# Later sums of squares for the norms behind the feed-forward blocks, and one set of squares for two norms between the layers

## The chip, the core and the metric

The kernel runs on one core of one Trainium2 chip. The metric is the device time of one execution in microseconds (us); the time before is the median of three runs. The core has five engines that work side by side, each through its own list of instructions in order: TensorE (PE in the profile, its weight loads PEld), VectorE (DVE), ScalarE (ACT), GpSimd (POOL) and SyncE (SP, which issues DMAs here; POOL issues some too). An instruction that waits for another engine holds up all that stands behind it on its own.

## The reference

Two layers over x of 512 tokens by 1024 features, in float32:

```
for l in range(2):
    x = x + 0.5 * swiglu(rms_norm(x, ffn1_norm[l]), gate1, up1, down1)     # "FFN1", inner width 2816
    h = rms_norm(x, mix_norm[l]); p = h @ w_in[l]                           # "mix": latent attention and a conv module
    x = x + concat(attention(p), conv(p)) @ w_out[l]
    x = x + 0.5 * swiglu(rms_norm(x, ffn2_norm[l]), gate2, up2, down2)     # "FFN2"
    x = rms_norm(x, post_norm[l])
rms_norm(x, g) = x * rsqrt(mean(x*x over features) + 1e-6) * g
```

Between the layers two norms follow each other: the post norm of layer 0 and the FFN1 norm of layer 1.

## The kernel before, in words

x lies in on-chip memory turned, as 8 tiles `x[:, m, :]` of 128 features by 512 tokens. Every float32 product is made of three cheaper ones of 512 (or 256) columns (`mm3`, lines 208 to 213): high part times high part, high times low, low times high. So each operand is split into a high part (an ACT cast, line 158 for a weight, 297 for a feed-forward quarter) and a low part (a DVE subtraction, lines 165 and 299). A weight arrives in a `raw` buffer by DMA, is cast, and its low part follows.

**Norms.** A product may start before the norm's factor is known: the operand is x times the gain (`split_scaled`, lines 223 and 224), and the products are multiplied by the factor afterwards. The factor takes these steps, in class `Stats` and its users:
- `add`: ACT squares an x tile (line 243; line 240 for the first, into the accumulator) and DVE or POOL adds it to the accumulator (line 247);
- `sums`: four one-column products on PE (line 254) sum the accumulator over the features;
- `token`: DVE scales the sums (`vtok`, line 261), POOL raises them to the power -0.5 (`rtok`, line 229); a first call of `norm()` does this much;
- `spread_sb`: four transposes on PE (line 270) spread the 512 factors over all partitions, an ACT copy (line 276) brings them to R; this is the second call of `norm()`.

Between the layers `NormPost` does it for two norms: it has two accumulators (st3 for x, st4 for x times the post gain), two sets of sums, a chain of small DVE and POOL steps (lines 1245 to 1251), and two spreads (R and Rp).

**A feed-forward block** (`ffn_body`) works on 11 pairs of inner column groups, in chunks (0,2), (2,5), (5,8), (8,11). Chunk 0 uses plain products: pair 0, then pair 1, each in two rows r, each row with two banks of PSUM (gate and up) of 24 products. When R is there, `plain_out` (lines 352 to 357) makes an activation of a row's two banks, split at lines 217 and 218; four activations come out of chunk 0. At the same time the generator `operands` (lines 375 to 388) prepares the operands of the other chunks on DVE and ACT. Chunk 0's down projection starts three blocks "ahead" with the first three activations. Chunks 1 to 3 use a seven-product scheme over three pairs each (`pair`, `down`), and the last `down` calls `done` for each finished x tile; the squares come behind that.

**The mix** (`mix_body`) starts with two groups of 24 products from the conv weights `wcv` (variable `first`), then one group from `wql` (step q0), then R, then the next conv groups (step c1, weights `wcv` again), and so on after the list `SEQ`.

**Order.** The program is recorded in the order of the code; a scheduler then sets each engine's order by its own timing, with a limited number of buffers per pool (7 PSUM banks). `tc.issue_after(i)` adds the condition that what is recorded under it stands behind instruction i on the same engine. `in_turn` (lines 181 to 184) keeps the low parts on DVE in their order by such a condition: `turns[V]` is the instruction behind which the next low part stands.

Of the kernel before, what the change touches and what calls it, by code (L numbers as in the profile page):

```python
# [12 lines left out]
ALU = mybir.AluOpType  # L13
# [48 lines left out]
WOG = 4  # L62
CHAIN = 400
WAKE = 10
KS = (0, 2, 4, 6, 1, 3, 5, 7)
WOP = 4
EVP = "DAD"
# [17 lines left out]
def encoder_kernel(ctx: ExitStack, tc: tile.TileContext, xT, consts, vecs, rgain, wgu1, wd1, wdq1,  # L85
# [21 lines left out]
    def bank():  # L107
        return psum.tile([P, S], FP, tag="ps", name=nm("ps"))
# [122 lines left out]
    class Stats:  # L231
# [5 lines left out]
        def add(self, src, scale=1.0, last=False, eng=None, apart=False, into=None):  # L237
            if self.acc is None:
                self.acc = slot() if into is None else into
                A.activation(self.acc, src, AF.Square, scale=scale)  # L240
                return
            sq = tmp() if into is None else into
            A.activation(sq, src, AF.Square, scale=scale)  # L243
            if apart:
                self.tail = sq
                return
            (eng or (V if last else G)).tensor_tensor(self.acc, self.acc, sq, ALU.add)

        def sums(self, made=bank):
            ps = made()  # L250
# [56 lines left out]
    def ffn_body(fpool, l, gx, norm, wgu, wd, wdq, wdr, gain, done, w0, halved, chunks, whole, late_rows):  # L307
# [52 lines left out]
        def after(name):  # L360
            return tc.issue_after(order[name]) if name in order else nullcontext()
# [199 lines left out]
        def advance(n):  # L561
            for _ in range(n):
                next(steps, None)

        for p0, p1 in chunks:
            f0, fn = 2 * p0, 2 * (p1 - p0)
            last = p1 == NF // 2
            short = last and p0 == CHUNKS[-1][0]
            act = held if short else []
            for p in range(p0, p1) if not short else ():  # L570
                if p == 0:
                    os = []
                    for r in range(2):
                        ws = w0[2 * r:2 * r + 2] if w0 else [load_w(wgu[l, p, 2 * r + q], WC) for q in range(2)]
                        os.append([bank(), bank()])
                        if w0 and not r:
                            plain_first(os[r], ws)
                        elif w0:
                            plain(os[r][:1], ws, range(KD))
                            plain([None] + os[r][1:], ws, range(KD // 2))  # L580
                            with tc.issue_after(order["mm"]):
                                norm()
                            with after("sums"):
                                plain([None] + os[r][1:], ws, range(KD // 2, KD))
                        elif late_rows:
                            for a, b in WHOLE:
                                plain(os[r], ws, range(a, b))
                                if r and a == 0:
                                    with tc.issue_after(order["mm"]):
                                        norm()  # L590
                            if r:
                                R = norm()
                        else:
                            plain(os[r], ws, range(KD - 1))
                            plain(os[r], ws, range(KD - 1, KD))
                            R = norm()
                    if not w0:
                        scaled(os, R)
                elif p < CHUNKS[0][1]:
                    for r in range(2):  # L600
                        ws = [load_w(wgu[l, p, 2 * r + q], WC) for q in range(2)]
                        o = [bank(), bank()]
                        if w0 and not r:
                            with tc.issue_after(order["mm"]):
                                plain(o[:1], ws, KS[:KD // 4])
                            with tc.issue_after(order["mm"]):
                                R = norm()
                            with after("spread"):
                                plain(o[:1], ws, KS[KD // 4:])
                                plain([None] + o[1:], ws, range(KD))  # L610
                            scaled(os, R)
                        else:
                            plain(o, ws, range(KD))
                        advance(8)
                        act.append(plain_out(o, R))
                else:
                    order.setdefault("pe", order["mm"])
                    act += pair(p, whole or not last)
            if p0 and (whole or not last):
                c = (p0 - CHUNKS[0][1]) // NP  # L620
                if p1 == CHUNKS[-1][0]:
                    held = pair(p1, False)
                down(act, (lambda g: wdq[l, g, c]) if p1 - p0 == NP else (lambda g: wdr[l, g]), done if last else None)
                continue
            ahead = {}
            if short:
                wide_w = [load_cols(wd, l, 4 * q, f0, fn) for q in range(2)]
            def block(m, queue=None):
                return load_w(wd[l, m, :, f0 * P:(f0 + fn) * P], fn * P, queue=queue)
            if p0 == 0:  # L630

                for m in range(3):
                    ahead[m] = bank(), block(m, G)
                    group(*ahead[m], act, range(fn - 1), fn)
                next_w = {3: block(3, G)}
            for m in range(halved if last else KD):
                if short:
                    pd = bank()
                    group(pd, part_w(wide_w, m, fn), act, range(fn), fn)
                elif m in ahead:  # L640
                    pd, w = ahead[m]
                    group(pd, w, act, range(fn - 1, fn), fn)
                else:
                    pd = bank()
                    w = next_w[m] if p0 == 0 else block(m)
                    group(pd, w, act, range(fn), fn)
                if p0 == 0 and m + 4 < KD:
                    next_w[m + 4] = block(m + 4, G)
                    if m == 0:
                        order["low"] = turns[V]  # L650
                if p0 == 0:
                    advance(2)
                    if norm.after:
                        with tc.issue_after(order["evicted"]):
                            norm.after(m)
                with after("low") if m in ahead and m else nullcontext():
                    order["evicted"] = V.scalar_tensor_tensor(x[:, m, :], pd, 0.5, x[:, m, :], ALU.mult, ALU.add).ins
                if last:
                    done(m)
            if last:  # L660

                ms = range(halved, KD)
                ws = [part_w(wide_w, m, fn) if short else load_w(wd[l, m, :, f0 * P:(f0 + fn) * P], fn * P) for m in ms]
                for h in range(2):
                    ts = slice(h * HS, (h + 1) * HS)
                    for m, w in zip(ms, ws):
                        pd = bank()
                        group(pd[:, 0:HS], w, act, range(fn), fn, ts)
                        V.scalar_tensor_tensor(x[:, m, ts], pd[:, 0:HS], 0.5, x[:, m, ts], ALU.mult, ALU.add)
                        done(m, h)  # L670
            if p0 == 0:
                advance(99)
# [10 lines left out]
            mix_body(kpool, l, gx, norm, done)  # L683

    def mix_body(kpool, l, gx, norm, done):
        u, order = [], {}
        diag = kpool.tile([P, PT, Q], FP, tag="m", name=nm("m"), bufs=11)
        G.tensor_tensor(diag, cst[:, None, CI32:CI32 + Q].to_broadcast([P, PT, Q]),
                        vv(l, "cp")[:, :, None].to_broadcast([P, PT, Q]), ALU.mult)
# [53 lines left out]
        ssk = small.tile([P, NT, H], FP, tag="ssk", name=nm("ssk"))  # L743

        def latent_q(j):
            ps = bank()
            group(ps, load_w(wql[l, j], WC, "q"), gx, range(KD), KD)
            pq.append(ps)

        def latent_q_out():  # L750
# [127 lines left out]


        first = groups([wcv[l, 0], wcv[l, 1]], gx, WHOLE)  # L880
        rm = norm()
        for step in SEQ.split():
            if step == "R":
                R = norm()
# [327 lines left out]
    for l in range(L):  # L1212
# [10 lines left out]
        if l + 1 < L:  # L1223
            nx, st4 = [], Stats()
            gc = tiny("gc", KD)
            G.tensor_tensor(gc, gp, vv(l + 1, "g1"), ALU.mult)

            def done2(m):
                nx.append(split_scaled(x[:, m, :], gc[:, m:m + 1]))
                for i in range(KD) if m == KD - 1 else ():  # L1230
                    with tc.issue_after(order["scaled"]):
                        st3.add(x[:, i, :], eng=V)
                        A.activation(x[:, i, :], x[:, i, :], AF.Copy, scale=gp[:, i:i + 1])
                        st4.add(x[:, i, :], eng=V)
            ffn(l, gx, norm2, wgu2, wd2, wdq2, None, vv(l, "g2"), done2, chunks=SHORT, whole=True)
            gx = nx

# [125 lines left out]
```

## Time and profile before

| | us |
|---|---|
| median of three runs (1743.22 to 1745.96) | 1745.44 |
| the profiled execution | 1745.87 |
| its span, first to last instruction | 1743.7 |
| PE busy in the span | 1723.4 (99%) |
| DVE / ACT / POOL busy | 1482.4 / 1111.3 / 365.0 |

Times in the profile count from the span's start. The 2.2 us between the execution's time and its span lie outside of the instructions. An engine's busy time is the union of its instructions; PE's instructions overlap their neighbours, so a busy PE is not a PE at its peak, and the granted clock (PEclk, 1.00 is full) has to be read beside it. The rows read "start, duration, engine, line, operation, out<-in, size", and a bracket tells how long the engine sat idle before and what released it.

### The profile page before, as it was taken

How to read it: one execution, taken by the hardware profiler on the slowest of the kernel's cores; microseconds unless marked ns; L12 is line 12 of the kernel's file. 1: busy time of each engine (PE TensorE's matmuls, PEld its weight loads, DVE VectorE, ACT ScalarE, POOL GpSimd, SP SyncE). 2: the span in 40 equal slices, each digit the busy share in tenths (PEclk: the TensorE clock that was granted, in tenths of full speed). 3: DMA queues.
4: the chain of work that ended last, by engine and by line, in shares of the span. 5: the costliest groups of instructions: out<-in, count | busy, mean ns of one | idle time of the engine just before them, and what ended most of it. 6: DMA issues, size and time to landing. Idle time of an engine off the chain costs nothing. (4 is left out here: it accounts for less than half of the span.)

```text
span 1743.7 us, 31890 instructions
## 1 busy us (share of the span) xinstructions
PE 1723.4 (99%) x12684; PEld 1586.6 (91%) x12684; DVE 1482.4 (85%) x2145; ACT 1111.3 (64%) x1727; POOL 365.0 (21%) x334
## 2 busy tenths in 40 slices
PE   9999999999999999999999999999999999999998
PEld 8899999888678899999979999998976788999997
DVE  7888989978965989898988989897989659888887
ACT  5576757557953576757755757675778435767564
POOL 2000000047823100010010011110576410011110
PEclk9999999999999999999999999999999999999999
DMA  5567575424303466676525575754251125675743
GB/s 184 146 154 196 134 201 132 141 73 120 75 25 103 115 166 173 160 176 160 137 74 156 133 199 132 202 132 132 83 151 32 51 83 149 157 190 138 199 110 100
DMA packets 73269, 234.21 MB, mean 134 GB/s; under 512 B 8736, under 2 KB 10912, under 8 KB 73120
## 3 DMA queue, kind: packets, MB, share of 16 engines
q1 hardware_dynamic: 51984, 163.48, 29.2%
q0 software_dynamic: 20992, 68.69, 21.8%
q8 instruction: 99, 1.62, 0.4%
q14 instruction: 50, 0.41, 0.1%
q10 hardware_dynamic: 144, 0.00, 0.0%
HBM read 227.95 MB, written 2.10 MB: 132 GB/s over the span
## 5 line engine op out<-in xcount | busy, mean ns | idle before, releaser
L211 PE MATMUL ps<-r,weights 128*128 128x256 f32 (+1 forms) x2680 | 819.2, 306 | 0.0
L210 PE MATMUL ps<-r,weights 128*128 128x256 f32 (+1 forms) x2680 | 814.8, 307 | 0.3 <-ACT weights L297 0.2
L212 PE MATMUL ps<-r,weights 128*128 128x256 f32 (+1 forms) x2400 | 739.1, 310 | 1.1 <-DVE weights L299 1.1
L210 PEld LDWEIGHTS ps<-r,weights 128*128 128x128 f32 x2680 | 504.9, 188 | 30.0 <-ACT weights L158 1.7
L211 PEld LDWEIGHTS ps<-r,weights 128*128 128x128 f32 x2680 | 505.0, 188 | 26.7 <-DVE r L224 0.2
L212 PEld LDWEIGHTS ps<-r,weights 128*128 128x128 f32 x2400 | 451.6, 188 | 30.3 <-DVE weights L299 1.5
L210 PE MATMUL ps<-xj,weights 128*128 128x256 f32 x864 | 238.5, 276 | 0.0
L211 PE MATMUL ps<-xj,weights 128*128 128x256 f32 x864 | 238.5, 276 | 0.0
L297 ACT CAST weights<-fr 128x1024 fp32r<-128x1024 f32 (+2 forms) x184 | 175.9, 956 | 90.3 <-DVE fr L452 44.9
L299 DVE TENSOR_TENSOR weights<-fr,weights 128x1024 fp32r<-128x1024 f32 (+2 forms) x184 | 203.8, 1107 | 31.1 <-ACT weights L297 31.1
L158 ACT CAST weights<-raw 128x1024 fp32r<-128x1024 f32 (+4 forms) x116 | 105.5, 922 | 165.7 <-PE ps L211 95.1
L432 POOL DMA_DIRECT2D ls<-in_wgu x72 | 62.9, 873 | 581.7 <-ACT ls L431 526.4
L165 DVE TENSOR_TENSOR weights<-raw,weights 128x1024 fp32r<-128x1024 f32 (+4 forms) x100 | 107.0, 1080 | 65.1 <-ACT weights L158 64.8
L210 PEld LDWEIGHTS ps<-xj,weights 128*128 128x128 f32 x864 | 162.2, 188 | 0.0
L211 PEld LDWEIGHTS ps<-xj,weights 128*128 128x128 f32 x864 | 162.2, 188 | 0.0
L212 PE MATMUL ps<-xj,ls 128*128 128x256 f32 x576 | 159.0, 276 | 0.0
L297 ACT CAST weights<-raw 128x1024 fp32r<-128x1024 f32 (+2 forms) x116 | 110.2, 950 | 45.6 <-DVE raw L535 26.6
L299 DVE TENSOR_TENSOR weights<-raw,weights 128x1024 fp32r<-128x1024 f32 (+2 forms) x116 | 127.8, 1101 | 12.9 <-ACT weights L297 12.5
L1028 POOL TENSOR_TENSOR y<-y,pr 128x495 f32<-128x495 f32 (+29 forms) x90 | 119.3, 1328 | 51.9 <-ACT pr L1026 46.6
L431 ACT ACTIVATE ls<-fr 128x1024 fp32r<-128x1024 f32 (+2 forms) x64 | 62.5, 976 | 103.8 <-PE ps L212 65.1
L519 DVE SCALAR_TENSOR_TENSOR x<-ps,x 128x512 f32<-128x512 f32 x168 | 115.1, 685 | 5.7 <-PE ps L212 4.9
L432 POOL DMA_DIRECT2D ls<-in_wdq x44 | 38.3, 871 | 343.1 <-ACT ls L431 326.3
(259 smaller groups left out, 3083.8 us busy)
## 6 DMA issues: line engine op xcount, KB each, us to landing
fr<-in_wgu SPq DMA_DIRECT2D x112, 512.0 KB, 4.6
ls<-in_wgu POOLq DMA_DIRECT2D x72, 512.0 KB, 7.3
raw<-in_wgu SPq DMA_DIRECT2D x62, 512.0 KB, 5.1
fr<-in_wdq SPq DMA_DIRECT2D x66, 384.0 KB, 4.8
ls<-in_wdq POOLq DMA_DIRECT2D x44, 384.0 KB, 6.2
raw<-in_wdq SPq DMA_DIRECT2D x22, 384.0 KB, 5.6
raw<-in_wd POOLq DMA_DIRECT2D x32, 256.0 KB, 3.1
raw<-in_wcv SPq DMA_DIRECT2D x16, 512.0 KB, 3.3
```

Of the source, the lines that this page charges most:

```text
L158: order["cast"] = in_turn("h", lambda: A.copy(hi[:, :w], raw[:, :w]))
L165: in_turn(e, lambda: e.tensor_tensor(lo[:, :w], raw[:, :w], hi[:, :w].bitcast(FP), ALU.subtract))
L210: T.matmul(o, lh, rh, start=first, stop=False, skip_group_check=free)
L211: T.matmul(o, lh, rl, start=False, stop=False, skip_group_check=free)
L212: order["mm"] = T.matmul(o, ll, rh, start=False, stop=last, skip_group_check=free).ins
L297: in_turn("h", lambda: A.copy(hi[:, :w], src[:, :w]))
L299: order["lo"] = in_turn(V, lambda: V.tensor_tensor(lo[:, :w], src[:, :w], hi[:, :w].bitcast(FP), ALU.subtract))
L431: A.activation(lo[:, :n], src[:, :n], AF.Copy, scale=-1.0)
L432: G.dma_start(out=lo[:, :n], in_=w, accum_op=ALU.add)
L519: return V.scalar_tensor_tensor(v, o.rearrange("p (m t) -> p m t", m=2), 0.5 * sign, v, ALU.mult, ALU.add).ins
L1028: order["conv"] = G.tensor_tensor(ys[c][:, s:], ys[c][:, s:], pr[:, s:], ALU.add).ins
```

## The change

Three places, one idea: the sums of a norm's squares stand further back in PE's order, with products of the next group ahead of them and behind them, before the spread.

- In the mix, `norm()` is no longer called after the two first conv groups. Step q0 records four of its eight k-steps (QS = 4, twelve products), then the sums behind them, then the other twelve, and the spread of step R follows. `turns[V] = summed` puts the low parts of all weights loaded after q0's behind the last addition of squares on DVE.
- In FFN1 of layer 1 (`late_rows`), the sums stand twelve products earlier than the end of pair 0 (after LS = 6 of 8 k-steps of row 1), and the spreads move from behind pair 0 into pair 1, behind 18 products of its first bank. `scaled` (the first two `plain_out` and the start of `operands`) follows there.
- Between the layers one set of ACT squares serves both accumulators: st4 adds the square times gp*gp (`add_scaled`, DVE). The second set of eight squares goes; the eight scalings of x by gp (line 1233) stay.

```diff
+QS = 4
+LS = 6
 class Stats:
     def add(...):
...
-            (eng or (V if last else G)).tensor_tensor(self.acc, self.acc, sq, ALU.add)
+            self.last = (eng or (V if last else G)).tensor_tensor(self.acc, self.acc, sq, ALU.add).ins
+            return sq
+
+        def add_scaled(self, sq, scale):
+            if self.acc is None:
+                self.acc = slot()
+                V.tensor_scalar(self.acc, sq, scale, None, ALU.mult)
+            else:
+                self.last = V.scalar_tensor_tensor(self.acc, sq, scale, self.acc, ALU.mult, ALU.add).ins
 ffn_body:
+        early = w0 or late_rows
...
                         elif late_rows:
                             for a, b in WHOLE:
-                                plain(os[r], ws, range(a, b))
-                                if r and a == 0:
+                                if r and a == LS:
                                     with tc.issue_after(order["mm"]):
                                         norm()
-                            if r:
-                                R = norm()
+                                with after("sums") if r and a == LS else nullcontext():
+                                    plain(os[r], ws, range(a, b))
...
-                    if not w0:
+                    if not early:
                         scaled(os, R)
...
-                        o = [bank(), bank()]
-                        if w0 and not r:
+                        o = [bank()]
+                        if not (late_rows and not r):
+                            o.append(bank())
+                        if early and not r:
+                            n = LS if late_rows else KD // 4
                             with tc.issue_after(order["mm"]):
-                                plain(o[:1], ws, KS[:KD // 4])
+                                plain(o[:1], ws, KS[:n])
                             with tc.issue_after(order["mm"]):
                                 R = norm()
+                            if late_rows:
+                                o.append(bank())
                             with after("spread"):
-                                plain(o[:1], ws, KS[KD // 4:])
+                                plain(o[:1], ws, KS[n:])
 mix_body, latent_q(j):
             ps = bank()
-            group(ps, load_w(wql[l, j], WC, "q"), gx, range(KD), KD)
+            w = load_w(wql[l, j], WC, "q")
+            if not j:
+                turns[V] = summed
+                group(ps, w, gx, range(QS), KD)
+                with tc.issue_after(order_of("product")):
+                    rm = norm()
+            with tc.issue_after(order_of("sums")) if not j else nullcontext():
+                group(ps, w, gx, range(0 if j else QS, KD), KD)
...
-        rm = norm()
+        rm, summed = None, norm.st.last
 between the layers:
+            gp2 = tiny("gp2", KD)
+            G.tensor_tensor(gp2, gp, gp, ALU.mult)
...
-                        st3.add(x[:, i, :], eng=V)
+                        sq = st3.add(x[:, i, :], eng=V)
+                        st4.add_scaled(sq, gp2[:, i:i + 1])
                         A.activation(x[:, i, :], x[:, i, :], AF.Copy, scale=gp[:, i:i + 1])
-                        st4.add(x[:, i, :], eng=V)
```

How the instructions stand then, at the places that the prediction speaks of (the changed file's lines are numbered from 2 on, in these functions 10 to 23, higher; L210, L211, L212 of before are L212, L213, L214 there).

PE at the start of the mix in layer 0, before: ps_3965 and ps_3966 are the banks of the two first conv groups, r_3902 the accumulator of squares, ps_4024 the bank of q0.

```order
L210 MATMUL ps_3966<-r_3898,weights 128x512
...
L212 MATMUL ps_3966<-r_3898,weights 128x512
L254 MATMUL ps_4016<-ones,r_3902 128x1 x4
L210 MATMUL ps_4024<-r_3869,weights 128x512
...
L212 MATMUL ps_4024<-r_3898,weights 128x512
L270 MATMUL ps_4053<-cst,rtok_4022 128x128 x4
```

The same place in the changed kernel; q0's bank is ps_4015.

```order
L214 MATMUL ps_3966<-r_3898,weights 128x512
L214 MATMUL ps_4015<-r_3873,weights 128x512
...
L214 MATMUL ps_4015<-r_3881,weights 128x512
L264 MATMUL ps_4033<-ones,r_3902 128x1 x4
L212 MATMUL ps_4015<-r_3885,weights 128x512
...
L214 MATMUL ps_4015<-r_3898,weights 128x512
L280 MATMUL ps_4053<-cst,rtok_4039 128x128 x4
```

The sums stood behind the last product of the first groups with all 24 of q0 between them and the spread; now twelve of q0's products stand ahead of the sums and twelve behind.

DVE at that place, before: r_3895 and r_3899 are the low parts of the last two x tiles, raw_4025 is q0's weight, raw_4069 and raw_4098 are c1's two weights, raw_4135 is q1's.

```order
L165 TENSOR_TENSOR weights<-raw_4025,weights 128x1024
L165 TENSOR_TENSOR weights<-raw_4069,weights 128x1024
L224 SCALAR_TENSOR_TENSOR r_3895<-x,vec,r_3894 128x512
...
L247 TENSOR_TENSOR r_3902<-r_3902,t_3904 128x512
...
L165 TENSOR_TENSOR weights<-raw_4098,weights 128x1024
L247 TENSOR_TENSOR r_3902<-r_3902,t_3922 128x512
L165 TENSOR_TENSOR weights<-raw_4135,weights 128x1024
L261 TENSOR_SCALAR vtok_4015<-ps_4016 128x4
```

The same place in the changed kernel; q0's weight is raw_4016 there.

```order
L167 TENSOR_TENSOR weights<-raw_4016,weights 128x1024
L226 SCALAR_TENSOR_TENSOR r_3895<-x,vec,r_3894 128x512
...
L249 TENSOR_TENSOR r_3902<-r_3902,t_3904 128x512
...
L249 TENSOR_TENSOR r_3902<-r_3902,t_3922 128x512
L167 TENSOR_TENSOR weights<-raw_4069,weights 128x1024
L167 TENSOR_TENSOR weights<-raw_4098,weights 128x1024
L167 TENSOR_TENSOR weights<-raw_4135,weights 128x1024
L271 TENSOR_SCALAR vtok_4032<-ps_4033 128x4
```

The low parts of c1's first weight, of its second and of q1's now all stand behind the seven additions and ahead of `vtok`.

PE in FFN1 of layer 1, before: ps_9850 is the last bank of pair 0, r_9721 and r_9724 the two accumulators, ps_9965 the first bank of pair 1.

```order
L212 MATMUL ps_9850<-r_9717,weights 128x512
L254 MATMUL ps_9876<-ones,r_9721 128x1 x4
L254 MATMUL ps_9887<-ones,r_9724 128x1 x4
L270 MATMUL ps_9921<-cst,rtok_9894 128x128 x4
L270 MATMUL ps_9928<-cst,rtok_9882 128x128 x4
L210 MATMUL ps_9965<-r_9688,weights 128x512
```

The same place in the changed kernel: ps_9838 is pair 0's last bank, ps_9917 pair 1's first.

```order
L214 MATMUL ps_9838<-r_9710,weights 128x512
L264 MATMUL ps_9876<-ones,r_9723 128x1 x4
L264 MATMUL ps_9887<-ones,r_9725 128x1 x4
L212 MATMUL ps_9837<-r_9715,weights 128x512
...
L214 MATMUL ps_9838<-r_9719,weights 128x512
L212 MATMUL ps_9917<-r_9690,weights 128x512
...
L214 MATMUL ps_9917<-r_9702,weights 128x512
L280 MATMUL ps_9936<-cst,rtok_9894 128x128 x4
L280 MATMUL ps_9943<-cst,rtok_9882 128x128 x4
L212 MATMUL ps_9917<-r_9710,weights 128x512
```

Between sums and spreads there was nothing; now there are the last twelve products of pair 0 and 18 of pair 1.

More of the change, by code (lines that the diff above doesn't have):

```diff
@@ L240, in add @@
                 A.activation(self.acc, src, AF.Square, scale=scale)
-                return
+                return self.acc
             sq = tmp() if into is None else into
@@ L685, in mix_body @@
     def mix_body(kpool, l, gx, norm, done):
-        u, order = [], {}
+        u, order, order_of = [], {}, ordered
         diag = kpool.tile([P, PT, Q], FP, tag="m", name=nm("m"), bufs=11)
@@ L745, in latent_q @@
         def latent_q(j):
+            nonlocal rm
             ps = bank()
-            group(ps, load_w(wql[l, j], WC, "q"), gx, range(KD), KD)
+            w = load_w(wql[l, j], WC, "q")
[6 more added lines that the diff above has]
+                group(ps, w, gx, range(0 if j else QS, KD), KD)
             pq.append(ps)
```

## The prediction, as it was put on record

> **What bounds the kernel now.** First the page's head, to see which engine is full; a change of 0.2% (3.5 us) is about what a measurement of this kernel can tell from none.
>
> ```profile
> span 1743.7 us, 31890 instructions
> PE 1723.4 (99%) x12684; PEld 1586.6 (91%) x12684; DVE 1482.4 (85%) x2145; ACT 1111.3 (64%) x1727; POOL 365.0 (21%) x334
> ```
>
> PE is the bound, idle for 20.3 us in all. Then the waits of PE alone (us in total, times, longest): three long ones, all at norms, and all at places that the diff touches.
>
> ```profile
> PE ps L254 <- DVE r L247: 4.9, 2, 2.5
> PE ps L270 <- DVE rtok L1251: 4.0, 1, 4.0
> PE ps L212 <- DVE weights L299: 1.1, 2, 0.9
> ```
>
> The first row is the sums at the start of the two mixes, waiting for the last addition of squares; the second the spread between the layers, waiting for the chain from sums to factor. The timeline of PE dates them, and gives the pace: 9 products from 883.73 to 885.77, 0.227 us each.
>
> ```profile
> 342.25 0.39 PE L212 MATMUL ps<-r,weights 128*128 128x512 f32 x1
> 345.09 1.84 PE L254 MATMUL ps<-ones,r 128*128 128x1 f32 x8 [2.46 <-DVE r L247]
> ...
> 883.73 0.39 PE L212 MATMUL ps<-r,weights 128*128 128x512 f32 x1
> ...
> 885.77 0.39 PE L212 MATMUL ps<-r,weights 128*128 128x512 f32 x1
> 886.00 1.84 PE L254 MATMUL ps<-ones,r 128*128 128x1 f32 x16
> 891.85 1.94 PE L270 MATMUL ps<-cst,rtok 128*128 128x128 f32 x8 [4.01 <-DVE rtok L1251]
> ...
> 1210.19 1.02 PE L254 MATMUL ps<-ones,r 128*128 128x1 f32 x8 [2.46 <-DVE r L247]
> 1211.07 0.49 PE L210 MATMUL ps<-r,weights 128*128 128x512 f32 x1
> ```
>
> Last the table by stretches (us, busy of PE, PEld, DVE, ACT, POOL with counts, then the granted clock), which shows what the idle time does not: behind each wait PE runs at half clock.
>
> ```profile
> 331.00:342.00 11.00, 11.00 (x55) 9.28 (x54) 10.69 (x14) 7.21 (x11) 0.20 (x1) 1.00 0.59 191
> 345.05:351.55 6.50, 6.46 (x19) 5.51 (x20) 1.61 (x5) 0.00 (x0) 1.04 (x1) 0.50 0.47 139
> 891.85:897.65 5.80, 5.80 (x18) 4.93 (x19) 4.06 (x7) 2.33 (x4) 0.00 (x0) 0.50 0.04 13
> 1211.70:1215.10 3.40, 3.40 (x10) 2.63 (x9) 0.17 (x2) 0.00 (x0) 0.82 (x1) 0.50 0.54 169
> 548.00:556.00 8.00, 8.00 (x41) 6.73 (x40) 2.56 (x3) 2.10 (x2) 2.58 (x2) 1.00 0.33 98
> ```
>
> So a wait costs its idle time and half of the stretch at 0.50: 2.46 + 6.50/2 = 5.7 us in the first mix, 4.01 + 5.80/2 = 6.9 between the layers, 2.46 + 3.40/2 = 4.2 in the second mix; 16.8 us in all, the most that the change can give. The last row is a norm whose sums already stand among products (FFN2 of layer 0): PE is busy throughout at clock 1.00. That is what the three places could become.
>
> [...]
>
> **The mix, part by part.** DVE and ACT there, then the chain behind the sums in layer 1:
>
> ```profile
> 334.27 2.36 DVE L165 TENSOR_TENSOR weights<-raw,weights 128x1024 fp32r<-128x1024 f32 x2
> ...
> 337.87 4.38 DVE L247 TENSOR_TENSOR r<-r,t 128x512 f32<-128x512 f32 x6
> 343.11 1.23 DVE L165 TENSOR_TENSOR weights<-raw,weights 128x1024 fp32r<-128x1024 f32 x1 [0.85 <-ACT weights L158]
> 344.26 0.69 DVE L247 TENSOR_TENSOR r<-r,t 128x512 f32<-128x512 f32 x1
> 355.65 1.23 DVE L165 TENSOR_TENSOR weights<-raw,weights 128x1024 fp32r<-128x1024 f32 x1 [7.21 <-ACT weights L158]
> ...
> 338.59 1.36 ACT L243 ACTIVATE t<-x 128x512 f32<-128x512 f32 x2 [1.65 <-DVE r L247]
> 342.04 1.99 ACT L158 CAST weights<-raw 128x1024 fp32r<-128x1024 f32 x2 [2.09 <-PE ps L211]
> ...
> 1211.25 0.16 DVE L261 TENSOR_SCALAR vtok<-ps 128x4 f32<-128x4 f32 x1
> 1211.49 1.04 POOL L229 TENSOR_TENSOR rtok<-vtok,minus_half 128x4 f32<-128x4 f32 x1 [15.19 <-DVE vtok L261]
> ```
>
> *Sums.* The seventh addition came at 344.26 only because the low part of a c1 weight stood ahead of it and waited for ACT; its square was there at 339.95. In the changed order it follows the sixth: done at 342.9. PE has products until 342.48, then twelve of q0 (2.7 us), and reaches the sums at 345.2. Margin 2.3 us, wait 0.
> *Spread.* The sums take 0.9 us (1210.19 to the next product at 1211.07), then twelve products: PE is at the spread at 348.8. Ahead of `vtok` DVE now has three low parts (start to start 1.15 us): from 342.9 to 346.5, with ACT's two casts shifted by about 1 us because PE ends the conv groups five products later. `vtok` at 346.6, POOL's 1.04 us, spread possible at 347.8. Margin 1.0; without cover, up to 1 us per mix.
> *c1's weights.* The first low part is delayed from about 335.4 to 342.9 and ends at 344.1; PE needs it behind the spread, at 349.3. Margin 5. What is queued behind on DVE has room: it idles 7.21 us before 355.65.
> *Queues.* SP's order does not change and no DMA is added; on POOL nothing moves here.
> The waits go with their half clock: 5.7 + 4.2 = 9.9 us.
>
> **Between the layers.**
>
> ```profile
> 869.84 1.41 DVE L224 SCALAR_TENSOR_TENSOR r<-x,gc,r 128x512 fp32r<-128x512 f32 x2
> 871.16 7.03 DVE L247 TENSOR_TENSOR r<-r,t 128x512 f32<-128x512 f32 x11
> 882.27 0.69 DVE L247 TENSOR_TENSOR r<-r,t 128x512 f32<-128x512 f32 x1 [0.61 <-ACT t L243]
> 887.51 0.15 DVE L261 TENSOR_SCALAR vtok<-ps 128x4 f32<-128x4 f32 x1
> 891.54 0.16 DVE L1251 TENSOR_TENSOR rtok<-rtok,rtok 128x4 f32<-128x4 f32 x1 [1.17 <-POOL rtok L229]
> ...
> L243 ACT ACTIVATE t<-x 128x512 f32<-128x512 f32 x9 | 5.4, 627 | 0.3
> ```
>
> *Arithmetic.* ACT loses 8 squares of about 0.63 us, 5.0 us off the path but what made the last addition late. DVE has 15 additions or multiplies instead of 14: 8 at 0.61 and 7 with a scalar at 0.67 (as L224), with two weights' low parts among them (2.3): 11.9 us from 871.2 on, so 883.1. POOL's one extra multiply of 8 columns stands at the program's start; its queue waits there for DMAs.
> *Sums.* They stand twelve products earlier: 886.00 - 2.7 = 883.3 for the first set (complete one step sooner, 882.4), 884.2 for the second (883.1). Margins 0.9 and 1.1, the thinnest here.
> *Spread.* Sums until 885.1; from `vtok` to the last step it took 4.2 us before, with a low part and two DMA issues between, now ahead or behind: at most 889.4. PE has 12 + 18 products (6.8 us): 891.9. Margin 2.5. On POOL two loads of down weights now stand behind the two power steps instead of ahead; their users come some 20 us later.
> So 6.9 us go. But **the spread comes when it came before** (891.85), and what hangs on R did not get faster, while PE is 18 products and a half clock further:
>
> ```profile
> 893.59 0.69 DVE L352 TENSOR_TENSOR t<-ps,r 128x512 f32<-128x512 f32 x1 [1.89 <-ACT r L276]
> ...
> 921.73 0.68 DVE L218 TENSOR_TENSOR r<-t,r 128x512 fp32r<-128x512 f32 x1
> ...
> 927.03 0.69 DVE L657 SCALAR_TENSOR_TENSOR x<-ps,x 128x512 f32<-128x512 f32 x1 [1.61 <-PE ps L212]
> ...
> 928.24 1.29 DVE L165 TENSOR_TENSOR weights<-raw,weights 128x512 fp32r<-128x512 f32 x2
> ```
>
> From R to the fourth activation DVE works 28.8 us without a break. In the changed order one block's low part (0.6) is gone from that stretch and the spread is 0.4 quicker at full clock: ready at 921.4. PE, from 892.8 (eight transposes, 0.9 us), has 78 products of pair 1, 36 of the down blocks with the first three activations and 4 high parts: it needs it at 919.5 and waits 1.9. Then the next down block's low part: 6.5 us behind the fourth activation before (928.9), of which DVE itself idled 1.6; so 926.3, and PE, 14 products on, is there at 924.6: 1.7 more. I take 3.5 us given back; the bounds are 0 (hidden cover) and 6.9 (the whole gain). Net 3.4 us.
>
> **Sum.** 5.7 + 4.2 + 3.4 = 13.3 us off the profiled execution's 1745.87: 1732.6. That execution is 0.4 above the median, so 1732.1 for a median.
>
> **Rivals.** (1) DVE hides all: 16.8 us kept, 1728.6. For it: in 893 to 922 PE never waited; against: the count of 118 products. (2) Between the layers nothing is left, by late sums (margins 0.9 and 1.1) or a half clock behind the new waits (3.5 us idle within 5 us, where 2.46 in a row were enough): 9.9 us gained, 1735.5.
> (3) The half clock in the mixes does not come from the waits: only 2.46 twice is won there, with 3.4 between the layers 8.3 us: 1737.1. Against it: the row of 548 to 556, sums without half clock. [...]
> (4) Slower: the low parts put behind the squares starve c1. If c1's first were as late as the low part that now comes at 355.65 (end 356.9), PE would wait 356.9 - 349.3 = 7.6 us and pay a half clock of 3.2, 10.8 in each layer; against 13.3 won that is 8.3 us slower, 1753.7. It decides from 6.6 us per layer on. Against it: DVE's 7 us of idle time there and a margin of 5 us.
> (5) Other stalls take its place at once: 1744 to 1746. Against it: the order shows the sums moved, and each margin is positive.
>
> **How the numbers follow.** Likeliest 0.62, own range 1730 to 1735; (1) 0.10; (2) 0.11; (3) 0.07; (4) 0.03; (5) 0.07. Faster by over 0.2% (below 1741.9): the likeliest, (1), (2), (3), 0.90, less 0.01 for mixtures of them with (5): 0.89. Within: 0.08. Slower: 0.03. The range goes from 1727.5 (rival 1 less 1 us for the spread of the runs) to 1739 (rival 3 and its 2 us): outside are (4), (5) and little else.
>
> **What would show it.** Right: no PE wait at the sums or spreads of the three places; clock 1.00 from 340 to 352 and at the second mix's start; new PE waits of 1 to 4 us in all some 25 to 35 us behind the double spread, released by DVE's L218 or the low part of a 512-column weight; the mixes' ends 5.7 and then 13 us earlier. Wrong: sums still waiting for an addition of squares, a stretch at 0.50 anywhere inside, or PE idle at c1.

## The result, and the profile after

The changed kernel takes 1754.23 us (median of six runs, 1753.46 to 1755.52) against 1745.70 for the kernel before: ratio 1.0052, 95% interval 1.0039 to 1.0065. It is 8.5 us slower; the forecast was 13.3 us faster, with the range ending at 1739.

The waits went as forecast. The page's head, then PE's six longest waits (us in total, times, longest):

```profile
span 1751.7 us, 31874 instructions
PE 1739.7 (99%) x12684; PEld 1603.9 (92%) x12684; DVE 1484.6 (85%) x2146; ACT 1107.0 (63%) x1719; POOL 364.6 (21%) x335
```

```profile
PE ps L213 <- DVE r L220: 1.2, 1, 1.2
PE ps L214 <- DVE weights L309: 1.1, 1, 1.1
PE ps L140 <- DVE ones L136: 1.1, 1, 1.1
PE ps L949 <- ACT r L957: 1.0, 2, 0.5
PE ps L214 <- DVE weights L167: 0.9, 1, 0.9
PE ps L212 <- ACT weights L1189: 0.7, 1, 0.7
```

The two rows of 4.9 and 4.0 us are gone, and none of the three norms that the diff touches waits any more. (Three waits of 0.2 to 0.3 us follow; two of them belong to the last norm of the kernel, which the diff leaves alone.) PE idles for 12.0 us instead of 20.3. The table by stretches (us, busy time of PE, PEld, DVE, ACT, POOL with counts, then the granted clock) shows the three places without a half clock:

```profile
345.00:360.00 15.00, 15.00 (x74) 12.51 (x73) 10.51 (x16) 6.78 (x9) 1.04 (x1) 1.00 0.35 115
895.00:910.00 15.00, 15.00 (x72) 12.51 (x71) 13.08 (x20) 5.41 (x10) 2.22 (x4) 1.00 0.25 71
1215.00:1235.00 20.00, 20.00 (x95) 16.65 (x95) 14.45 (x21) 9.67 (x12) 1.03 (x1) 1.00 0.34 106
```

But PE is busy for 1739.7 us where it was busy for 1723.4, with the same 12684 products and with less half clock in them. The extra time lies in no place that the diff touches. Here are two stretches in the middle of feed-forward blocks, of the kernel before and then of the changed one:

```profile
100.00:150.00 50.00, 50.00 (x443) 49.94 (x442) 46.10 (x66) 33.59 (x50) 5.17 (x6) 1.00 0.63 156
700.00:750.00 50.00, 50.00 (x443) 50.00 (x443) 42.08 (x57) 36.12 (x54) 5.23 (x6) 1.00 0.61 151
```

```profile
100.00:150.00 50.00, 50.00 (x434) 50.00 (x433) 44.76 (x65) 32.56 (x49) 5.15 (x6) 1.00 0.63 154
700.00:750.00 50.00, 50.00 (x432) 50.00 (x431) 40.83 (x56) 35.02 (x50) 4.32 (x5) 1.00 0.63 158
```

Both times PE is busy without a gap at clock 1.00, and yet it gets through 434 and 432 products instead of 443. The first stretch ends some 200 us ahead of the first moved sums. Asked for the tile `xj` alone (duration of one product, min/median/max in ns), the two traces differ in every product that reads it; before, then after:

```profile
L210 PE MATMUL ps<-xj,weights x864: 276/276/276, 76.6 to 1695.6; 128*128 128x256 f32 x173
L212 PE MATMUL ps<-xj,ls x576: 276/276/276, 76.8 to 1695.8; 128*128 128x256 f32 x192
```

```profile
L212 PE MATMUL ps<-xj,weights x864: 278/282/285, 76.8 to 1703.9; 128*128 128x256 f32 x173
L214 PE MATMUL ps<-xj,ls x576: 276/278/282, 77.1 to 1704.1; 128*128 128x256 f32 x192
```

The durations of 0.28 us overlap, so what counts is the step from start to start. The timeline of PE in the changed kernel shows five steps in 0.59 us, 0.118 each, where the kernel before steps at 0.113 with the same tiles:

```profile
708.57 0.28 PE L212 MATMUL ps<-xj,weights 128*128 128x256 f32 x1
708.68 0.28 PE L213 MATMUL ps<-xj,weights 128*128 128x256 f32 x1
708.80 0.28 PE L214 MATMUL ps<-xj,ls 128*128 128x256 f32 x1
708.92 0.28 PE L212 MATMUL ps<-xj,weights 128*128 128x256 f32 x1
709.03 0.28 PE L213 MATMUL ps<-xj,weights 128*128 128x256 f32 x1
709.16 0.28 PE L214 MATMUL ps<-xj,ls 128*128 128x256 f32 x1
```

What is new in every block is an address. `gp2 = tiny("gp2", KD)` takes 32 bytes per partition in the pool `small`, which keeps two buffers of each tile. Everything allocated behind that pool lies 64 bytes higher in SBUF (the on-chip memory): among it, of the feed-forward blocks, the operands `xj` and `xs`, the low parts `ls` and the weight quarters `fr`. The tiles ahead of it, `r` and `weights`, stay. Places below are those of the compiled programs; no view of the profile prints them. A "step" is the mean from one product's start to the next in the trace, over 256-column products of the tiles named.

### The profile page after: what moved, and what is told of

Same layout as the page of the kernel before. It is cut to its first block, busy times and chain, and to the rows that moved or that the text cites. A ratio compares the mean times of both kernels' runs of the same rounds, so it can differ in the third digit from the quotient of the medians.

```text
span 1751.7 us, 31874 instructions
## 1 busy us (share of the span) xinstructions
PE 1739.7 (99%) x12684; PEld 1603.9 (92%) x12684; DVE 1484.6 (85%) x2146; ACT 1107.0 (63%) x1719; POOL 364.6 (21%) x335
## 3 DMA queue, kind: packets, MB, share of 16 engines
q0 software_dynamic: 20992, 68.69, 21.9%
## 4 chain that ended last, share of the span: by engine, by line
PE 89%; DVE 5%; ACT 3%; issue 1%; DMA 1%; POOL 0%; SPq 0%; DVEq 0%; ACTq 0%; POOLq 0%
PE ps L212 29%; PE ps L214 28%; PE ps L213 28%; PE ps L994 1%; ACT pr L1049 1%; PE ps L972 1%; ACT r L957 1%; DVE r L386 1%; DVE t L391 1%; DVE cv L1045 1%; DMA raw<-in_wd 1%; PE ps L949 0%; DVE mx L953 0%; PE ps L987 0%; DVE xj L386 0%
## 5 line engine op out<-in xcount | busy, mean ns | idle before, releaser
L213 PE MATMUL ps<-r,weights 128*128 128x256 f32 (+1 forms) x2680 | 819.9, 306 | 1.2 <-DVE r L220 1.2
L212 PE MATMUL ps<-r,weights 128*128 128x256 f32 (+1 forms) x2680 | 814.8, 308 | 1.0 <-ACT weights L1189 0.7
L214 PE MATMUL ps<-r,weights 128*128 128x256 f32 (+1 forms) x2400 | 737.9, 310 | 2.0 <-DVE weights L309 1.1
L212 PEld LDWEIGHTS ps<-r,weights 128*128 128x128 f32 x2680 | 503.3, 188 | 30.7 <-ACT weights L160 2.9
L213 PEld LDWEIGHTS ps<-r,weights 128*128 128x128 f32 x2680 | 504.9, 188 | 27.9 <-DVE r L220 1.6
L214 PEld LDWEIGHTS ps<-r,weights 128*128 128x128 f32 x2400 | 450.3, 188 | 30.9 <-DVE weights L167 2.2
L212 PE MATMUL ps<-xj,weights 128*128 128x256 f32 x864 | 243.6, 282 | 0.0
L213 PE MATMUL ps<-xj,weights 128*128 128x256 f32 x864 | 243.4, 282 | 0.0
L212 PEld LDWEIGHTS ps<-xj,weights 128*128 128x128 f32 x864 | 162.6, 188 | 0.0
L213 PEld LDWEIGHTS ps<-xj,weights 128*128 128x128 f32 x864 | 162.5, 188 | 0.0
L214 PE MATMUL ps<-xj,ls 128*128 128x256 f32 x576 | 160.2, 278 | 0.0
```

What stands on the lines that cost most here:

```text
L212: T.matmul(o, lh, rh, start=first, stop=False, skip_group_check=free)
L213: T.matmul(o, lh, rl, start=False, stop=False, skip_group_check=free)
L214: order["mm"] = T.matmul(o, ll, rh, start=False, stop=last, skip_group_check=free).ins
```

## The experiments

**Is it the place?** Theory: the 64 bytes. Rival: the moved work itself, or a PE that is slower because its clock no longer falls. In the kernel, `GAP` is the width of an unused tile in `small`, so it moves what lies behind without touching any work.

```diff
-GAP = 72
+GAP = 56      # changed kernel: the 64 bytes of gp2 taken back
```

> The changed kernel with the unused tile at the head of the small tiles' pool made 64 bytes shorter, which is what the new tile gp2 (two buffers of 32 bytes) added; all tiles behind it then lie where they lay before the change. Theory position: the changed kernel is slow because the moving tiles xj and xs now begin at the same place in 128 bytes as the weights do, and each product of 256 columns that reads such a pair takes 117 to 121 ns instead of 113 to 114. Summed over the trace by pairs: 1440 products of xj with weights by 5.4 ns, 576 by 6.5, 432 of xs by 4.1, 557 of r with the low parts' tile by 4.3, and 5394 of r that follow such ones by 1.3 on average, 23 us in all; so this kernel takes 1754.2 - 23 = 1731 us (1727 to 1736), 440 or more products in 50 us of FFN, PE busy near 1716. Rival work: the slower products come from the moved sums and squares or from the clock that is never lowered; then nothing changes: 1752 to 1756.

Measured: 1732.36 us (1731.13 to 1733.22) against 1744.02 for the kernel before, ratio 0.9932 (0.9917 to 0.9947). Head and a stretch of its page:

```profile
span 1731.5 us, 31874 instructions
PE 1717.9 (99%) x12684; PEld 1581.1 (91%) x12684; DVE 1483.3 (86%) x2146; ACT 1107.0 (64%) x1719; POOL 365.2 (21%) x335
```

```profile
700.00:750.00 50.00, 50.00 (x444) 50.00 (x443) 44.61 (x64) 35.77 (x52) 4.36 (x5) 1.00 0.56 132
```

21.9 us of time and 21.8 us of PE's busy time go with the 64 bytes, and 444 products fit in the stretch again. The same shift the other way round, in the kernel before:

```diff
-GAP = 72
+GAP = 88      # kernel before
```

> The kernel before, its order and its work untouched, with the unused tile 64 bytes longer, so that the tiles behind it lie where they lie in the changed kernel. Theory position: the 23 us come on top, 1745.7 + 23 = 1769 us (1764 to 1772), 433 to 435 products in 50 us of FFN. Rival work: no change, 1743 to 1747.

Measured: 1766.59 us, ratio 1.0129 (1.0114 to 1.0145), 22.6 us more with no instruction changed. `xj` has the changed kernel's durations:

```profile
L210 PE MATMUL ps<-xj,weights x864: 278/282/285, 77.3 to 1717.2; 128*128 128x256 f32 x173
```

So the shift costs about 22 us with or without the moved sums, and the rival falls.

**Which tile, and what place?** The theory was that a product is slow when its moving tile (`r`, `xj`, `xs`, the first name behind the arrow) and its stationary one (`weights`, `ls`, the second) begin at the same place in 128 bytes. Two kernels on the changed one: `ls` and `fr` alone put back, and a shift of 32 bytes instead of 64.

```diff
-        fpool.tile([P, 48], FP, tag="gap", name=nm("gap"), bufs=1)
+        fpool.tile([P, 32], FP, tag="gap", name=nm("gap"), bufs=1)   # e3: between xs and ls
-GAP = 72
+GAP = 64   # e4
```

> The changed kernel with the gap between xs and ls 64 bytes shorter: ls and fr lie as before the change, xj and xs stay moved, so that xj, xs, ls and the weights all begin at 0 in 128 bytes and r at 64. Theory equal position (any moving tile against any stationary one): the 557 products of r with ls get their speed back, the 1152 of xj beside ls lose it: 1748 to 1755 us. Rival low parts: it is the moved ls and fr (read by VectorE and ScalarE too) that cost: 1730 to 1736.

> The changed kernel with the unused tile 32 bytes shorter: xj and xs begin at 96, ls at 32 in 128 bytes, the weights at 0, r at 64: no moving tile begins where a stationary one does. Theory equal position: full speed, 1729 to 1736 us. Rival any shift: only the place before the change is good, 1745 to 1756. Rival coarse: what counts is the position in 32 bytes, all equal here and in every other kernel: no difference between the four, 1754.

Measured: 1753.83 us (ratio 1.0055, 1.0040 to 1.0070) and 1753.74 (1.0058, 1.0041 to 1.0074). The first is as the theory has it: products of `r` with `ls` fall from a step of 117.8 ns to 113.2, those of `xj` with `ls` rise from 114.0 to 118.7. The second refutes it: no moving tile begins at the place of a stationary one there, and `xj` with the weights still steps at 118.4. Equal places are not the rule. That any shift is slow, its rival, is still possible; n1 and n2 below test it.

The next theory was a distance of 64 bytes, counted in 128. If so, a shift by a whole 128 bytes (m4) does nothing, and moving the weights instead of `xj` (m5) is as bad.

```diff
-GAP = 72
+GAP = 24           # m4, on the changed kernel: 128 bytes below the place before
...
-WOFF = 16, 48
+WOFF = 0, 32       # m5, on the realigned kernel: 256-column weights 64 bytes lower
...
```

> The changed kernel with the unused tile 192 bytes shorter: all tiles behind it lie 128 bytes lower than before the change. Theory distance (full speed where the moving and the stationary tile begin 64 bytes apart, counted in 128): xj and xs at 64, ls at 0, weights at 0, all as before: 1729 to 1736 us. Rival, the place counts in more than 128 bytes: some products of xj slow again, 1740 to 1755.

> The realigned kernel with the weights of the 256-column products placed 64 bytes lower (an offset inside their own tile, 0 and 32 elements instead of 16 and 48; the tile's size is kept), so that they begin at 64 in 128 bytes, as r, xj and xs do; nothing else moves. Theory distance: 5684 products of r, 2016 of xj and 432 of xs go from 113.4 to 119.2 ns, 8132 x 5.8 = 47 us: 1779 us (1770 to 1786). Rival, the place of xj and xs by itself: no change, 1732.

Measured: 1751.15 us (1.0032, 1.0020 to 1.0044): 18.8 us over the realigned kernel, so the theory falls: 128 bytes of distance do count. And 1777.86 (1.0186, 1.0172 to 1.0200), 45.5 us over the realigned kernel where 47 were forecast. The stationary side counts as the moving one does: the step is 119 ns in m5, as it is for the moved `xj` in the changed kernel. Nor does the other engines' work set the pace there: sorted by what was at work beside them (200 to 1700 us, steps under 140 ns), m5's products of `r` and `xj` with `weights` step at 119.0 ns with VectorE alone, 118.9 with ScalarE alone and 119.4 with no other compute engine (27 products), and at 118.8 with fewer than five DMA packets under way. The same stretch of m5:

```profile
700.00:750.00 50.00, 50.00 (x423) 50.00 (x423) 40.87 (x52) 33.70 (x46) 4.33 (x5) 1.00 0.62 158
```

After m4 two readings stood: places count by themselves in 256 bytes, or only the distance between tiles counts. On the realigned kernel, a constant of 128 or 256 bytes goes from the pool in front of `r` and `weights` into `small` (n1: everything 128 bytes lower; n2: `r` and `weights` 256 bytes lower, `xj`, `xs` and `ls` unmoved).

```diff
-    mneg = cpool.tile([P, 64], BF, name="mneg")
+    mneg = small.tile([P, 64], BF, tag="mneg", name="mneg", bufs=1)   # n1, with GAP = 24
...
-    mrow = cpool.tile([P, P], BF, name="mrow")
+    mrow = small.tile([P, P], BF, tag="mrow", name="mrow", bufs=1)    # n2, with GAP = 56
```

> The realigned kernel with every tile of the ring, the weights and the blocks 128 bytes lower (a constant of 128 bytes, mneg, goes from the constants' pool to the small one, whose unused tile gives up as much), all distances between them kept. In the run with xj alone 128 bytes lower xj began at 64 in 256 bytes, as 64 in 128 as before, and its products took 117.5 to 119 ns all the same. Theory own place: a moving tile that begins at 64 in 256 is slow, one at 192 fast, against weights at 0 or 128; then all 8980 products of 256 columns are slow here, about 4.6 ns each, 41 us: 1773 us (1765 to 1782). Theory relation: only how the tiles lie to each other counts, xj to the weights or to r; then nothing changes: 1729 to 1736 us.

> The realigned kernel with the ring and the weights 256 bytes lower and xj, xs and ls where they were (a constant of 256 bytes, mrow, goes from the constants' pool to the small one). Theory 256: positions count in 256 bytes; no pair changes: 1729 to 1736 us. Rival, the period is longer (512 or more): the 3024 products of xj and xs, now 256 bytes further from the weights, or the 5960 of r get slow: 1745 us or more.

Measured: 1732.05 us (0.9919, 0.9903 to 0.9936) and 1731.60 (0.9914, 0.9899 to 0.9929). Both runs have 444 products in 700 to 750 us, as the realigned kernel has, against 432 in m4. So in these runs the place of a tile does not count by itself, its distance to the others does, and 256 bytes more of distance change nothing. `xj` in m4 and in n1 begins at the same place; `weights` (and `r`) do not. m4, then n1:

```profile
L212 PE MATMUL ps<-xj,weights x864: 278/279/280, 76.6 to 1702.1; 128*128 128x256 f32 x173
```

```profile
L212 PE MATMUL ps<-xj,weights x864: 276/276/276, 77.3 to 1682.3; 128*128 128x256 f32 x173
```

What is left to tell m4 from the realigned kernel: counted from the weights to the moving tile in 256 bytes, the high parts lie at 192 and the low parts at 64 in the realigned kernel, and the other way round for `xj` in m4. Two kernels (n3, n4) set these distances by the weights' offsets alone.

```diff
-WOFF = 16, 48
+WOFF = 48, 80      # n3, with GAP = 24: high 64, low 192
...
+WOFF = 16, 16      # n4, with GAP = 56: high 192, low 192
...
```

> The realigned kernel with the 256-column weights 128 bytes higher inside their own tile (offsets 48 and 80 elements instead of 16 and 48; the unused tile gives back what the weights' tile grew, so xj, xs, ls and r stay). Counted in 256 bytes from the weights to the moving tile, the high parts go from 192 to 64 and the low parts from 64 to 192: for xj what it was in the run that moved everything behind the unused tile by 128 bytes, and now for r too. Theory distance in 256: that is a slow arrangement, 8980 products by 4.5 ns, 40 us: 1772 us (1760 to 1785). Rival, xj against r is what counted there: nothing changes, 1729 to 1736.

> The realigned kernel with the low parts' weights at the offset of the high ones (16 elements for both), so that both are 192 in 256 bytes from r, xj and xs; ls stays at 64. Theory runs of 64: slow are two loads in a row at distance 64 (the high parts in the slow arrangement of 128 bytes), two at 192 are not; full speed, 1729 to 1736 us. Rival: loads have to alternate between 192 and 64; then the products around the low parts get slow, a third to all of 8130 by 4.5 ns: 1745 to 1770.

Measured: 1772.56 us (1.0148, 1.0123 to 1.0173; 1772 was forecast) and 1732.42 (0.9932, 0.9915 to 0.9948). In products from 100 to 150 us and from 700 to 750 us, the weights at 192 ran at full pace, also many in a row (n4: 444 and 443); one in three at 64 cost nothing (the realigned kernel: 442 and 444); two in three at 64 (the high parts serve two products each) were slow in m4 (436 and 432) and, from 149 us on, in n3 (443 and 424; see the last section). Distances of 0 and 128 (changed kernel and e2: 434 and 432; m5: 423 and 423) and of 32, 96 and 224 (e4: 434 and 432) were slow too.

**What the three edits bring.** With the place out of the way, the forecast's terms can be measured: the mixes alone on the kernel before (m1), and the changed kernel without `gp2` and its single set of squares (m3: two sets on ACT again, nothing moved in SBUF).

```diff
+            if not j:                         # m1: latent_q as in the change, the rest as before
+                turns[V] = summed
+                group(ps, w, gx, range(QS), KD)
+                with tc.issue_after(order_of("product")):
+                    rm = norm()
...
+                        st4.add(x[:, i, :], eng=V)        # m3: as before the change
-                        sq = st3.add(x[:, i, :], eng=V)
-                        st4.add_scaled(sq, gp2[:, i:i + 1])
+                        st3.add(x[:, i, :], eng=V)
...
-            gp2 = tiny("gp2", KD)
-            G.tensor_tensor(gp2, gp, gp, ALU.mult)
```

> The kernel before with the change's part in the two mixes alone (sums behind twelve products of q0, low parts of c1 and q1 behind the additions); no tile is added, so nothing moves in SBUF. Theory parts: the mixes bring what the product-by-product comparison of the realigned run shows there, 5.70 us in the first and 4.3 in the second: 10.0 us less than before, ratio 0.9943. Rival: part of the mixes' gain is owed to the earlier end of the layer before (its low parts come sooner): 5.7 to 8 us less.

> The changed kernel without its third edit: between the layers two sets of squares on ScalarE again, as before the change, and no gp2, so that all tiles lie where they lay. Theory idle edit: the last addition ended at 882.96 before the change and the moved sums come at 886.00 - 2.7 = 883.3, so even two sets are in time; same as the realigned kernel within 1.5 us, ratio to before 0.9924 to 0.9941. Theory needed edit: the last square of ScalarE is late for sums that come twelve products earlier; PE waits 1 to 2 us there and its clock is halved for some us: 2 to 5 us above the realigned kernel, ratio 0.9945 to 0.9965.

Measured: 1735.21 us, ratio 0.9941 (0.9929 to 0.9953), 10.0 less than the kernel before in the same batch (1745.25), as forecast; of the norms' three waits only the spread between the layers is left:

```profile
PE ps L271 <- DVE rtok L1260: 4.0, 1, 4.0
```

And 1732.14 us, ratio 0.9922 (0.9908 to 0.9935): the third edit brings nothing. The timeline of DVE without it shows why; its last addition of squares waits for ACT and is still in time, since the step behind the sums waits for PE, not for it:

```profile
879.68 0.69 DVE L249 TENSOR_TENSOR r<-r,t 128x512 f32<-128x512 f32 x1 [0.61 <-ACT t L245]
881.65 0.16 DVE L271 TENSOR_SCALAR vtok<-ps 128x4 f32<-128x4 f32 x1 [1.28 <-PE ps L264]
```

That version, the changed kernel less its third edit, beats both kernels with no number touched by hand: it has no tile to pay for.

## Why the prediction was wrong

**The step that failed** is the one on `gp2`, "POOL's one extra multiply of 8 columns stands at the program's start". It priced the instruction and not the tile that it writes. Behind it stands an assumption that the sum never names: that the other products keep their pace. No rival had the products themselves slower; the only slower one, (4), was starved weights at c1, and PE never waited there. The missed term is +22 us (1754.23 less 1732.36), against 13.3 us of forecast gain. That (4) gives 1753.7 us, close to the 1754.23 measured, is a coincidence.

The trace before held a hint that I passed over. 24 products of 256 columns at the kernel's end read weights at another offset (64 in 128 bytes, as `r`), and step at 0.12 us:

```profile
1727.52 0.28 PE L210 MATMUL ps<-r,weights 128*128 128x256 f32 x1
1727.64 0.28 PE L211 MATMUL ps<-r,weights 128*128 128x256 f32 x1
1727.76 0.28 PE L212 MATMUL ps<-r,weights 128*128 128x256 f32 x1
1727.88 0.28 PE L210 MATMUL ps<-r,weights 128*128 128x256 f32 x1
```

The code held another: an unused tile of 72 columns and two odd offsets for the weights.

**The other terms** can be read from the realigned kernel, by the start of the same product, counted from the first, in its trace and in the trace before (us, realigned less before):

| place | ahead | behind | change | forecast |
|---|---|---|---|---|
| first mix | +0.41 | -5.29 | -5.70 | -5.7 |
| between the layers, spread | -5.22 | -12.04 | -6.82 | -6.9 |
| fourth activation, next down block | -12.04 | -8.81 | +3.23 | +3.5 |
| second mix | -7.83 | -12.14 | -4.31 | -4.2 |

Each is within 0.3 us. The give-back has the two places named ahead; the timeline of PE in the realigned kernel shows both waits, the activation and a down block's low part:

```profile
915.77 0.50 PE L213 MATMUL ps<-r,weights 128*128 128x512 f32 x1 [1.16 <-DVE r L220]
920.59 0.50 PE L214 MATMUL ps<-r,weights 128*128 128x512 f32 x1 [0.81 <-DVE weights L167]
```

The price of a wait, its idle time and half of the stretch at 0.50, was right at the three places (the table's 5.70, 6.82 and 4.31 us), but it was not what decided. That 1732.36 us comes so near to 1732.1 is in part luck. The four terms add up to 13.6 us and small delays elsewhere took some back: the spans differ by 12.2, and the medians by 11.7 in that batch. In n1, n2 and n4, with the same three edits at full pace, the medians differ by 14.4, 14.9 and 12.6.

The trace before also shows where two equal waits of 2.46 us differ in cost: the granted clock stays at 0.50 for 6.83 us in the first (344.72 to 351.55) and for 3.41 in the second (1211.71 to 1215.12). In the first it fell during the wait itself, ahead of the sums at 345.09.

**The rivals.** (1), all 16.8 us kept, falls by the give-back; (2), nothing left between the layers, by the 3.6 us net there (6.82 less 3.23); the medians of m1 and m3, from one batch, differ by 3.1. (3), that the mixes' half clock does not come from the waits, falls by m1: 10.0 us, not the 4.9 of two waits of 2.46 alone. (5) falls: no stall took a removed one's place beyond the 3.23 us. The third edit, which was to end the squares earlier, brought no time (m3).

## What to carry to other kernels

A new tile can move every tile allocated behind it (here by 64 bytes, at 21.9 us); compare the addresses of the two builds before pricing the instructions. Where PE is full, compare products per stretch at equal clock first (443 against 434 in 50 us): a pace that changes, without a wait, in stages the edit does not touch was here no matter of order or waits (e2: 22.6 us more with no instruction changed). And an edit that only adds margin, as the third here, should be tried without before its costs are accepted.

## What was not expected of the hardware

From one 256-column product to the next it took 113 ns in the kernel before and, in the mean of a pair of tiles, 119.0 (`xj` with the weights), 117.8 (`r` with `ls`) and 117.4 (`xs` with the weights) in the changed one, at granted clock 1.00 and with PE busy throughout. In these runs the step goes by how the moving tile lies to the weights, counted in 256 bytes (700 to 750 us: 443 or 444 products in n1, n2 and n4, 432 in m4, 423 in m5). Products of 512 columns with weights and `r` at the same place in 256 bytes step at 227 ns in the kernel before, about twice 113, while the 24 shorter ones shown above step at 120 with the same tiles at that distance.

The slow pace does not go by the pair alone. In the changed kernel three or six products of `r`, whose own distances are good, stay slow behind each run of `xj` (steps of 117 to 124 ns in 700 to 760 us, then 113 or 114). And in n3, whose distances are the same from the first block on, the stream ran at full pace until 149 us, stepped late once, and was slow in every later stretch read that is full of 256-column products (424 in 50 us, from 150 to 300 and from 650 to 850 us):

```profile
100.00:150.00 50.00, 50.00 (x443) 49.95 (x442) 46.12 (x66) 33.60 (x51) 5.16 (x6) 1.00 0.63 155
150.00:200.00 50.00, 50.00 (x424) 50.00 (x423) 40.18 (x51) 31.72 (x43) 5.18 (x6) 1.00 0.67 174
```

Its runs also spread most, 1764.11 to 1774.68 us. That late product starts at 149.29 us, just behind the end of its low part on VectorE (149.23), and two full-pace kernels have it too: in the kernel before and in the realigned one the step to it is 136 ns and the one behind it 222; the nine steps after these take 115 to 123 ns, and then the stream is back at 113. So behind that late product the steps are slow at good distances as well, but there the pace was back within about ten products; in n3 it was not. Why the distance decides, no run shows; the distances that no run had are open.
